# The first norm's modulation and the even layer's by matmuls on quarters of TensorE's columns, and two directions' scores on halves of its rows

## The chip, the cores and the metric

The kernel runs on one core of a Trainium2 chip. The metric is the device time of one execution in microseconds, taken as the median of several runs. The core has five engines that work side by side, each through its own instructions in their order: TensorE (PE), which multiplies a stationary block of weights of up to 128x128 with moving columns and writes to PSUM, VectorE (DVE), ScalarE (ACT), GpSimd (POOL) and SyncE (SP), which here issues all transfers between DRAM and the on-chip memory. An instruction that waits for another engine or for a transfer holds up all that is behind it on its engine.

## The reference

One step of a small trunk with two layers over 128 context tokens (tile 0 of the kernel) and 512 latent tokens (tiles 1 to 4), 1024 features, all in float32. The even layer has gated linear attention (GLA) and retention heads, the odd one latent attention; each is followed by a squared-ReLU MLP. Every norm is modulated: a shift, a scale and a gate come from the conditions `c` (latents) and `c_ctx` (context).

```python
def ada_mod(cond, w_ada, b_ada):
    m = jnp.einsum('bd,de->be', jax.nn.silu(cond), w_ada) + b_ada
    return jnp.split(m[:, None, :], 6, axis=-1)       # shift, scale, gate of the mixer; the same of the MLP

def pre_norm_mod(x, g, shift, scale):
    return rms_norm(x, g) * (1.0 + scale) + shift
```

So for each of 2 layers x 6 parts a vector of two conditions by 1024 features meets a matrix of 1024 x 1024: much weight to load, little to compute. In a chunk of a GLA head, with decayed queries and keys of 64 features, the scores are masked by direction:

```python
        a = jnp.where(causal_in_chunk, jnp.einsum('bhik,bhjk->bhij', q_dec, k_inv), 0.0)
        o = jnp.einsum('bhik,bhkv->bhiv', q_dec, S) + jnp.einsum('bhij,bhjv->bhiv', a, vi)
```

The scan runs forward and backward, each direction with its own decays, and the two outputs are added.

## The kernel before

Tokens lie in five tiles of 128. A product in float32 accuracy is made of three one-pass products: each operand is split into two summands (`hi`, `lo`; in the trace `wh` and `wl` for weights, and two `hT` for the normed, transposed input), and `mm3` issues hi x hi, hi x lo and lo x hi. Splitting a block of weights takes a copy on ACT and a subtraction on POOL or DVE. Some small products are done in plain float32 in one instruction, which the trace shows as two records, each with its own weight load.

The order of every engine's instructions is fixed when the program is written out. The kernel's parts are generators ("threads"). Class `Weave` runs them against a rough clock for each engine: `Engine.way` gives each instruction a duration from its size, and `_issue` gives a free engine the instruction of the lowest priority number, then the one that could have started longest ago. What it assumes decides only the order; on the chip an engine takes its instructions in that order and waits where an operand is late. SP's queue is filled in the same way, so a transfer that has to wait for room holds up those behind it. All instructions are emitted from one line (266 before the change), so groups in the trace are told apart by the names of their tiles.

The start. `ada_first` makes the first shift and scale (parts 0 and 1), in two halves of 512 features. `FIRST_LOADS` orders the loads: 16 of w_ada (`rada`, 256 rows x 512 columns each, scale and shift in turn), the tiles of x, and the first weights. PE takes all rows of the shift and the last four blocks of 128 rows of the scale: matmuls with four columns of weights (`wide`, the conditions among zeros) and 512 moving columns of w_ada. DVE takes the scale's first four blocks (`FIRST_ON_VECTOR`), as running sums `ada` on 128 partitions for each condition, which PE then sums by columns of ones. The four rows of the result go by ACT into `row`, four transposes put them on columns, and DVE makes `mod` of them. Behind each half `pre_norm` scales the transposed tiles (`h`, `hT`), and `gemm_first` begins the even layer's first product (bank `pg`) on that half of the features, for all five tiles, and then on the second half.

The even layer. `gemm_nat` makes the product's seven groups of columns, one after another, tile by tile. For each tile a `tile_thread` takes the banks as they come: gates and decays (`gk`, `la`, `pos`, `tri`), decayed queries and keys `qt` and `kt`, the masked scores, sums and states, GLA's gate `ga`, then retention (`dup`, `qk`, `qr`, `kr`) and its gate `gb`. For the GLA scores the forward direction's 64 features lie on the first 64 partitions and the backward ones on the other 64. For each direction four matmuls (one for each head) on 64 rows fill a bank, and DVE copies it under the mask (`copy_predicated`).

Beside it the thread `modulations` makes the parts that come next: `ADA_EVEN` are the even layer's gate and the MLP's shift and scale, (0,2), (0,3) and (0,4). Each has two halves; for each half `ada_half` has 16 DVE operations on 128x512 (`ada<-rada,cT,ada`), two for each block of 128 rows, and `ada_cols` two transposes and two sums on DVE, one PE matmul with `fold` (tile `pc<-sums,fold`), four small ACT copies and `mod`. The loads for it (`rada`, 256 KB) have two slots in the even layer. The other parts, `ADA_MLP` and `ADA_LAST`, are made in the same way beside the two MLPs.

`out_proj` is the even layer's output product with its norm and residual (`y`, `x`), and the MLP follows.

Of the kernel before, what the change touches and what calls it, by code (L numbers as in the profile page):

```python
# [11 lines left out]
F32 = mybir.dt.float32  # L12
# [7 lines left out]
P = 128  # L20
# [15 lines left out]
NCONST = 1320  # L36


def _constants():
# [4 lines left out]
    # running sums of log decays over a tile, taken from its middle (the 1/16 of the gate is in here)  # L44
# [20 lines left out]
    c[:, C_FOLD:] = j % 32 == np.arange(32)  # L65
# [4 lines left out]
# The parts of the kernel are generators that emit instructions; they are interleaved by a rough  # L70
# clock per engine, so that each engine's instructions come in the order in which their operands do.
# [5 lines left out]
class Slots:  # L77
    """The tiles of a tag (or of several pools), handed out and given back."""
# [16 lines left out]
class Weave:  # L95
    """Each thread's instructions come in their order; an engine that is free takes, of those that could start,
    the one of the lowest priority number, then the one that has waited longest (the vector engine: the
    one of the oldest thread)."""
# [55 lines left out]
    # the order  # L154
# [9 lines left out]
    def _at(self, th, eng):  # L164
        """When what the thread's next instruction needs is there."""
# [6 lines left out]
    def _end(self, th, eng, us):  # L172
        """When that could be through on this engine, behind those that go first."""
# [4 lines left out]
    def _advance(self, th):  # L178
        """To the thread's next instruction, or to what it waits for."""
# [30 lines left out]
    def _issue(self, eng, start):  # L210
# [3 lines left out]
        # rather idle for a moment than be in the way of what is more urgent  # L214
# [43 lines left out]
class Engine:  # L258
    """An engine of nc whose instructions also move its rough clock."""
# [38 lines left out]


class Either:  # L300
    """Whichever of some engines is through with it first."""
# [20 lines left out]
class Trunk:  # L322
# [31 lines left out]
    def at_last(self, left, do):  # L354
        """do() when the last of left[0] comes here."""
# [11 lines left out]
    def split(self, hi, lo, src, eng=None):  # L367
        """src == hi + lo, both in the tensor engine's one-pass float32 format."""
# [9 lines left out]
    def rsqrt(self, m, r, t, scale, post=1.0):  # L378
        """r = post * (scale * m) ** -0.5, with a Newton step behind exp(-ln / 2)."""
# [13 lines left out]
    def weight(self, src, shape, lo="vector", pair=False, quota=None, room=None, prio=1):  # L393
        """To be brought in as its two summands, in the order of these calls."""
# [4 lines left out]
    def weights(self):  # L399
        """Their loads; weight_rooms() finds room for the summands."""  # L400
# [64 lines left out]
    def gemm_nat(self, units, n, out, ready=None, done=None):  # L465
        """One group of columns, tile by tile of tokens: sets out[t] to the bank."""
# [20 lines left out]
    def gemm_first(self, units, n, out, ready):  # L487
        """The same, all tiles with the first half of the rows, then all with the second."""
# [25 lines left out]
    def ada_loads(self, parts, slots, nk=1, ahead=16, after=None):  # L514
        """The rows of w_ada behind ada_half(), nk * 128 at a time."""
# [39 lines left out]
    def ada_cols(self, l, sec, half, acc, res, room=None):  # L555
        """The sums over all rows, on columns."""
# [10 lines left out]
        nc.tensor.matmul(ps[0:32, 0:32], self.fold, sm.rearrange("p c b -> p (c b)"), start=True, stop=True)  # L567
        yield
        col = sm.rearrange("p c b -> p (c b)")[:, 0:8].rearrange("p (c j) -> p c j", c=2)
        pv = ps[0:32, 0:32].rearrange("p (c j b) -> p c j b", c=2, b=4)  # L570
        for b in range(4):
            nc.scalar.copy(col[32 * b:32 * b + 32], pv[:, :, :, b])
# [52 lines left out]
    def ada_first(self, mod, halves, prepared, x_go, c_go):  # L625
        """The first shift and scale, which all else waits for, by halves of their features: the columns of w_ada
        meet cond on the tensor engine, some of its rows on the vector engine."""
        nc, w = self.nc, self.w
        res = [self.mod_tile(sec) for sec in range(2)]
        # shift's conditions in the first two columns, scale's in the next two, and columns of ones for scale's sums  # L630
        wide, hd = yield from self.take(self.tmp, [P, 512], F32, "wide")
        wide = wide[:, 0:72].rearrange("p (k c) -> p k c", c=4)
        nc.vector.memset(wide, 0.0)
        for c in range(2):
            nc.vector.memset(wide[:, 16 + c, 2 + c:3 + c], 1.0)
# [16 lines left out]
        def by_vector(half, n, done):  # L652
            acc = yield from self.ada_half(0, 1, half, 0.0, n)
            w.set(done, acc)

        w.spawn(load())
        yield prepared
        for sec in range(2):
            nc.vector.tensor_copy(wide[:, sec * KC:sec * KC + KC, sec * 2:sec * 2 + 2],
                                  self.cT.rearrange("p (c k) -> p k c", c=2))  # L660
        for half in range(2):
            ps, hp = yield from self.bank()
            row, hw = yield from self.take(self.tmp, [P, 512], F32, "row")
            n = FIRST_ON_VECTOR[half]
            done = Event()
            if n:
                w.spawn(by_vector(half, n, done))
# [8 lines left out]
            if n:  # L676
                acc = yield done
                for c in range(2):
# [1343 lines left out]
```

## Time and profile before

| | |
|---|---|
| median of 3 runs | 1617.75 us (1616.5 to 1625.09) |
| profiled execution, first to last instruction | 1615.8 us |
| PE busy | 1529.0 us (95%), 8583 records |
| PE weight loads busy | 1338.8 us (83%) |
| DVE busy | 1051.6 us (65%), 1915 instructions |
| ACT, POOL busy | 634.0 us (39%), 397.4 us (25%) |
| mean TensorE clock granted | 0.977 |
| DMA | 166.12 MB, 103 GB/s on average |

The profiled execution has no other time of its own than its span. The ends of matmuls are modelled and matmuls are pipelined, so the distance from one start to the next tells what one costs, not its own duration. In a row of the timeline the first number is the start in us from the span's beginning, the second the length in us; x2 means two records merged, and what stands in brackets is the idle time of the engine before it and what ended it. In a row of groups the numbers behind the bar are the sum in us and the mean in ns of one, then the idle time before them. The engines' waits give the sum in us, the number and the longest.

### The profile page before, as it was taken

How to read it: one execution, taken by the hardware profiler on the slowest of the kernel's cores; microseconds unless marked ns; L12 is line 12 of the kernel's file. 1: busy time of each engine (PE TensorE's matmuls, PEld its weight loads, DVE VectorE, ACT ScalarE, POOL GpSimd, SP SyncE). 2: the span in 40 equal slices, each digit the busy share in tenths (PEclk: the TensorE clock that was granted, in tenths of full speed). 3: DMA queues.
4: the chain of work that ended last, by engine and by line, in shares of the span. 5: the costliest groups of instructions: out<-in, count | busy, mean ns of one | idle time of the engine just before them, and what ended most of it. 6: DMA issues, size and time to landing. Idle time of an engine off the chain costs nothing. (4 is left out here: it accounts for less than half of the span.)

```text
span 1615.8 us, 22873 instructions
## 1 busy us (share of the span) xinstructions
PE 1529.0 (95%) x8583; PEld 1338.8 (83%) x8583; DVE 1051.6 (65%) x1915; ACT 634.0 (39%) x1485; POOL 397.4 (25%) x317
## 2 busy tenths in 40 slices
PE   5999988889999999999997989999899999999997
PEld 1587767777888998998896989998799989988996
DVE  5577898885577778768748788884766333333335
ACT  2473433354532322332235556664543223222332
POOL 2423644432111211211136320012212112111213
PEclk9999999999999999999998999999999999999999
DMA  8323423333265454445322301113344222222211
GB/s 307 106 64 109 121 85 114 102 117 96 73 178 163 143 147 142 137 144 150 116 61 84 97 21 27 40 40 118 104 130 130 72 74 68 90 79 66 78 53 65
DMA packets 146733, 166.12 MB, mean 103 GB/s; under 512 B 12112, under 2 KB 92480, under 8 KB 146624
## 3 DMA queue, kind: packets, MB, share of 16 engines
q1 hardware_dynamic: 146624, 164.68, 33.8%
q8 instruction: 67, 1.10, 0.3%
q14 instruction: 42, 0.34, 0.1%
HBM read 158.69 MB, written 5.96 MB: 102 GB/s over the span
## 5 line engine op out<-in xcount | busy, mean ns | idle before, releaser
L266 PE MATMUL p<-hT,wh 128*128 128x256 f32 (+1 forms) x2048 | 444.3, 309 | 0.0
L266 PE MATMUL p<-wh,hid 128*128 128x512 f32 x1280 | 401.8, 392 | 0.0
L266 PEld LDWEIGHTS p<-hT,wh 128*128 128x128 f32 x2048 | 342.6, 188 | 1.4
L266 PE MATMUL p<-hT,wl 128*128 128x256 f32 (+1 forms) x1024 | 316.6, 309 | 0.0
L266 POOL TENSOR_TENSOR r<-r 128x384 f32<-128x384 f32 (+1 forms) x128 | 133.6, 1044 | 725.8 <-ACT hid L266 725.8
L266 PEld LDWEIGHTS p<-wh,hid 128*128 128x128 f32 x1280 | 241.8, 189 | 49.2
L266 PE MATMUL pg<-wh,hT 128*128 128x512 f32 (+3 forms) x840 | 269.4, 394 | 3.9 <-ACT hT L266 3.5
L266 ACT CAST wh<-raw 128x1024 fp32r<-128x1024 f32 (+3 forms) x169 | 172.3, 1026 | 251.2 <-PE p L266 243.3
L266 PE MATMUL p<-wl,hid 128*128 128x512 f32 x640 | 251.1, 392 | 0.0
L266 DVE SCALAR_TENSOR_TENSOR ada<-rada,cT,ada 128x512 f32<-128x512 f32 x292 | 238.7, 859 | 2.6 <-DMA rada<-in_w_ada 2.4
L266 DVE TENSOR_TENSOR wl<-raw,wh 128x1024 fp32r<-128x1024 f32 x121 | 148.3, 1225 | 89.5 <-ACT wh L266 88.3
L266 PEld LDWEIGHTS p<-hT,wl 128*128 128x128 f32 x1024 | 193.4, 189 | 0.2
L266 PEld LDWEIGHTS pg<-wh,hT 128*128 128x128 f32 x840 | 158.0, 194 | 37.9 <-issue 8.1
L266 DVE TENSOR_TENSOR y<-y,p 128x512 f32<-128x512 f32 x140 | 95.9, 685 | 104.7 <-PE p L266 104.5
L266 DVE TENSOR_TENSOR hid<-r,hid 128x384 fp32r<-128x384 f32 (+1 forms) x128 | 63.9, 500 | 152.6 <-POOL r L266 152.6
L266 ACT ACTIVATE r<-p 128x384 f32<-128x384 f32 (+1 forms) x128 | 56.1, 439 | 266.5 <-PE p L266 266.3
L266 POOL TENSOR_TENSOR wl<-raw,wh 128x1024 fp32r<-128x1024 f32 (+3 forms) x44 | 105.1, 2400 | 211.1 <-ACT wh L266 184.0
L266 PE MATMUL pg<-wl,hT 128*128 128x512 f32 (+3 forms) x360 | 145.8, 405 | 1.1 <-POOL wl L266 1.1
L266 PEld LDWEIGHTS p<-wl,hid 128*128 128x128 f32 x640 | 120.9, 189 | 24.2
L266 PEld LDWEIGHTS pg<-wl,hT 128*128 128x128 f32 x360 | 70.2, 195 | 16.3 <-issue 2.6
L266 ACT ACTIVATE hid<-r 128x384 fp32r<-128x384 f32 (+1 forms) x128 | 60.4, 472 | 2.2
L266 PE MATMUL ps<-kn,qn 128*128 128x320 f32 (+1 forms) x216 | 49.7, 311 | 1.4 <-ACT prob L266 1.4
(259 smaller groups left out, 2013.8 us busy)
## 6 DMA issues: line engine op xcount, KB each, us to landing
raw<-in_w_mlp SPq DMA_DIRECT2D x128, 512.0 KB, 4.2
rada<-in_w_ada SPq DMA_DIRECT2D x160, 256.0 KB, 2.9
rada<-in_w_ada SPq DMA_DIRECT2D x16, 512.0 KB, 5.4
raw<-in_w_in_even SPq DMA_DIRECT2D x16, 512.0 KB, 3.7
x<-in_x_sample SPq DMA_DIRECT2D x8, 512.0 KB, 7.7
gate<-gate SPq DMA_DIRECT2D x8, 512.0 KB, 4.6
raw<-in_w_out_even SPq DMA_DIRECT2D x8, 512.0 KB, 3.9
raw<-in_w_out_odd SPq DMA_DIRECT2D x8, 512.0 KB, 4.2
```

The lines of the kernel that those rows point to most:

```text
L266: emit = lambda: real(*a, **k)
```

## The change

Three things are changed.

First, the modulation in `ada_first` and that of `ADA_EVEN` no longer use DVE for the products. `wide` is now a constant tile of 34 columns for each block of rows, with the two conditions in columns 2 and 3 and zeros elsewhere. A window of 32 columns puts the conditions on rows 0 and 1 or on rows 2 and 3 of a quarter of the bank. `ada_four` issues four float32 matmuls in one piece, for four blocks of rows, each into another 32 partitions of the same bank, and so on another quarter of PE's columns. A half of a part takes two such batches, a half of the first shift and scale four. `ada_turned` copies the whole bank to `row` and adds the quarters up with four matmuls by `fold`, which is now 128 columns wide (ones where the row and column agree by 32). The loads of the even layer's parts have four slots and no longer two.

Second, the scores of both directions, eight matmuls on 64 rows, are issued in one piece, head by head with the two halves of the rows in turn, into two banks. The masked copies follow.

Third, the room for DVE's running sums (`pada`) is taken within the MLPs alone. `ada_cols`, which the MLPs still use, follows the wider `fold`. The order of all instructions is planned anew, with 1.4 us assumed for a batch of `ada_four` and 2.2 us for eight scores.

```diff
+    def batch(self, fn, calls, us):
+        ways = [self.way(fn, a, k) for a, k in calls]
+        self.w.put((self.name, us, lambda: [x[2]() for x in ways]))
...
+    def ada_four(self, ps, rows, start, stop):
+        self.nc.tensor.batch("matmul", [
+            ((ps[32 * j:32 * j + 32], self.wide[:, kc, 2 - 2 * sec:34 - 2 * sec], raw), dict(start=start, stop=stop))
+            for j, (raw, kc, sec) in enumerate(rows)], 1.4)
+
+    def ada_turned(self, ps, n, row):
+        nc = self.nc
+        nc.scalar.copy(row, ps)
+        yield
+        for j in range(4):
+            nc.tensor.matmul(ps[:, n * j:n * j + n], row[:, j * P:(j + 1) * P], self.fold[:, 0:n], start=True, stop=True)
+        yield
+
+    def ada_tensor(self, l, sec, half, res):
+        ps, hp = yield from self.bank()
+        for k0 in (0, 4):
+            got, held = [], []
+            for kc in range(k0, k0 + 4):
+                raw, hr = yield self.ada_ev[l, sec, half][kc]
+                got.append((raw, kc, 0))
+                held += hr
+            self.ada_four(ps, got, k0 == 0, k0 == 4)
+            self.drop(*held)
+            yield
+        row, hr = yield from self.take(self.tmp, [P, 512], F32, "row")
+        yield from self.ada_turned(ps, 2, row)
+        self.drop(hr)
+        self.mod_cols(l, sec, res[:, :, half * 4:half * 4 + 4], half * 4,
+                      ps[:, 0:8].rearrange("p (j c) -> p c j", c=2))
+        self.drop(hp)
...
         for half in range(2):
+            if (l, sec) in ADA_EVEN:
+                yield from self.ada_tensor(l, sec, half, res)
+                continue
             acc = yield from self.ada_half(l, sec, half, rest)
             yield from self.ada_cols(l, sec, half, acc, res)
...
-            todo = [(sec, kc) for kc in range(KC) for sec in range(2) if sec == 0 or kc >= n]
-            # one group for all columns of the bank
-            for sec, kc in todo:
-                raw, hr = yield self.ada_ev[0, sec, half][kc]
-                nc.tensor.matmul(ps[0:4], wide[:, sec * KC + kc], raw, start=(sec, kc) == todo[0],
-                                 stop=n == 0 and (sec, kc) == todo[-1])
-                self.drop(*hr)
+            todo = [(k0, sec) for k0 in (0, 4) for sec in (1, 0)]
+            for i, (k0, sec) in enumerate(todo):
+                got, held = [], []
+                for kc in range(k0, k0 + 4):
+                    raw, hr = yield self.ada_ev[0, sec, half][kc]
+                    got.append((raw, kc, sec))
+                    held += hr
+                self.ada_four(ps, got, i == 0, i == 3)
+                self.drop(*held)
                 yield
-            if n:
-                acc = yield done
-                for c in range(2):
-                    nc.tensor.matmul(ps[0:4], wide[:, 16 + c], acc[c], start=False, stop=c == 1)
-                yield
-            nc.scalar.copy(row[0:4], ps[0:4])
-            for j in range(4):
-                nc.tensor.transpose(ps[:, 4 * j:4 * j + 4], row[0:4, j * P:(j + 1) * P], self.ident[0:4, 0:4])
-            yield
+            yield self.cols_ready
+            yield from self.ada_turned(ps, 4, row)
...
-        self.ada_later(ADA_EVEN, self.slots(ph, "erada", 2))
+        self.ada_later(ADA_EVEN, self.slots(ph, "erada", 4))
...
+            pas = []
+            for _ in range(2):
+                pas.append((yield from self.bank()))
+            rows_ = [slice(d * 64, d * 64 + 64) for d in range(2)]
+            cols_ = [slice(h * P, (h + 1) * P) for h in range(NH)]
+            nc.tensor.batch("matmul", [((pas[d][0][:, c], kt[r, c], qt[r, 0, c]), dict(start=True, stop=True))
+                                       for c in cols_ for d, r in enumerate(rows_)], 2.2)
+            yield
             for d, M in ((0, A), (1, B)):
-                r = slice(d * 64, d * 64 + 64)
-                pa, hp = yield from self.bank()
-                for h in range(NH):
-                    s = slice(h * P, (h + 1) * P)
-                    nc.tensor.matmul(pa[:, s], kt[r, s], qt[r, 0, s], start=True, stop=True)
-                yield
-                nc.vector.copy_predicated(h4(M), masks[:, d].unsqueeze(1).broadcast_to((P, NH, P)), h4(pa))
-                self.drop(hp)
+                nc.vector.copy_predicated(h4(M), masks[:, d].unsqueeze(1).broadcast_to((P, NH, P)), h4(pas[d][0]))
+                self.drop(pas[d][1])
                 yield
```

More of the change, by code (lines that the diff above doesn't have):

```diff
@@ L35 @@
     0, 128, 256, 384, 512, 640, 768, 896, 1024, 1152, 1280, 1288)
-NCONST = 1320
+NCONST = 1416
 def _constants():
@@ L64, in _constants @@
     c[64:, C_POS + 3] = 1.0 / 16.0
-    c[:, C_FOLD:] = j % 32 == np.arange(32)
+    c[:, C_FOLD:] = j % 32 == i % 32
     return c
@@ L566, in ada_cols @@
         ps, hp = yield from self.take(self.psg if room else self.psum, [P, 512], F32, "pc")
-        nc.tensor.matmul(ps[0:32, 0:32], self.fold, sm.rearrange("p c b -> p (c b)"), start=True, stop=True)
+        nc.tensor.matmul(ps[:, 0:32], self.fold, sm.rearrange("p c b -> p (c b)"), start=True, stop=True)
         yield
         col = sm.rearrange("p c b -> p (c b)")[:, 0:8].rearrange("p (c j) -> p c j", c=2)
-        pv = ps[0:32, 0:32].rearrange("p (c j b) -> p c j b", c=2, b=4)
+        pv = ps[:, 0:32].rearrange("p (c j b) -> p c j b", c=2, b=4)
         for b in range(4):
-            nc.scalar.copy(col[32 * b:32 * b + 32], pv[:, :, :, b])
+            nc.scalar.copy(col[32 * b:32 * b + 32], pv[32 * b:32 * b + 32, :, :, b])
         self.drop(hp)
@@ L629, in ada_first @@
         res = [self.mod_tile(sec) for sec in range(2)]
-        wide, hd = yield from self.take(self.tmp, [P, 512], F32, "wide")
-        wide = wide[:, 0:72].rearrange("p (k c) -> p k c", c=4)
-        nc.vector.memset(wide, 0.0)
-        for c in range(2):
-            nc.vector.memset(wide[:, 16 + c, 2 + c:3 + c], 1.0)
+        nc.vector.memset(self.wide, 0.0)
         def load():
@@ L650, in load @@
             w.set(self.loaded)
-        def by_vector(half, n, done):
-            acc = yield from self.ada_half(0, 1, half, 0.0, n)
-            w.set(done, acc)
         w.spawn(load())
         yield prepared
-        for sec in range(2):
-            nc.vector.tensor_copy(wide[:, sec * KC:sec * KC + KC, sec * 2:sec * 2 + 2],
-                                  self.cT.rearrange("p (c k) -> p k c", c=2))
+        nc.vector.tensor_copy(self.wide[:, :, 2:4], self.cT.rearrange("p (c k) -> p k c", c=2))
         for half in range(2):
@@ L663, in ada_first @@
             row, hw = yield from self.take(self.tmp, [P, 512], F32, "row")
-            n = FIRST_ON_VECTOR[half]
-            done = Event()
-            if n:
-                w.spawn(by_vector(half, n, done))
-            todo = [(sec, kc) for kc in range(KC) for sec in range(2) if sec == 0 or kc >= n]
-            for sec, kc in todo:
-                raw, hr = yield self.ada_ev[0, sec, half][kc]
-                nc.tensor.matmul(ps[0:4], wide[:, sec * KC + kc], raw, start=(sec, kc) == todo[0],
-                                 stop=n == 0 and (sec, kc) == todo[-1])
-                self.drop(*hr)
-                yield
-            if n:
-                acc = yield done
-                for c in range(2):
-                    nc.tensor.matmul(ps[0:4], wide[:, 16 + c], acc[c], start=False, stop=c == 1)
-                yield
-            nc.scalar.copy(row[0:4], ps[0:4])
-            for j in range(4):
-                nc.tensor.transpose(ps[:, 4 * j:4 * j + 4], row[0:4, j * P:(j + 1) * P], self.ident[0:4, 0:4])
-            yield
+            todo = [(k0, sec) for k0 in (0, 4) for sec in (1, 0)]
[7 more added lines that the diff above has]
+                self.drop(*held)
+                yield
+            yield self.cols_ready
+            yield from self.ada_turned(ps, 4, row)
             pv = ps[:, 0:16].rearrange("p (j s c) -> p s c j", s=2, c=2)
-            yield self.cols_ready
             for sec in range(2):
@@ L692, in ada_first @@
             self.drop(hp, hw)
-        self.drop(hd)
     def pre_norm(self, t, x, xn, sm, mods, ready, halves=None, lo="gpsimd"):
@@ L776, in run @@
         self.pmod = self.pool(ctx, "mod", 2)
-        self.pada = self.pool(ctx, "ada", 1)
         self.sm = self.slots(ctx, "small", 20)
@@ L791, in run @@
         self.ident = const("ident", [P, P])
-        self.fold = const("fold", [P, 32])
+        self.fold, self.wide = const("fold", [P, P]), const("wide", [P, KC, 34])
         self.cT, self.cols = const("cT", [P, 16]), const("cols", [P, 160])
@@ L885, in main @@
                 load(post[16:32], k_rows("norm_mlp_post")),
-                load(self.fold, io["consts"][:, C_FOLD:C_FOLD + 32]), then=lambda at: w.set(arrived2, None, at))
+                load(self.fold, io["consts"][:, C_FOLD:C_FOLD + P]), then=lambda at: w.set(arrived2, None, at))
         yield arrived
@@ L985, in mlp @@
         NB = FF // 512
+        self.pada = self.pool(ph, f"ada{l}", 1)
         self.ada_later(ADA_MLP if l == 0 else ADA_LAST, self.slots(ph, f"rada{l}", 4))
@@ L1971 @@
 FIRST_LOADS = "aacaaaxaawaxaxaaxaaxaaa"
-FIRST_ON_VECTOR = (4, 4)
 ADA_EVEN = [(0, 2), (0, 3), (0, 4)]
```

## The prediction

> **What bounds the kernel now.** I read the page first, then the busy time by stretch, then what TensorE (PE) waits for.
>
> ```profile
> span 1615.8 us, 22873 instructions
> ```
>
> ```profile
> 0.00:64.00 64.00, 46.29 (x118) 12.62 (x119) 31.85 (x78) 17.66 (x35) 18.43 (x16) 0.95 0.71 237
> 64.00:440.00 376.00, 341.45 (x1798) 286.14 (x1796) 285.79 (x470) 173.08 (x404) 146.67 (x103) 0.94 0.33 97
> 440.00:1610.00 1170.00, 1141.28 (x6671) 1040.05 (x6669) 731.62 (x1364) 443.20 (x1046) 231.60 (x198) 0.99 0.33 97
> ```
>
> After the stretch come its length and busy us of PE, weight load, VectorE (DVE), ScalarE (ACT) and GpSimd (POOL), then PE's clock, the DMA share and GB/s. PE sets the end everywhere. The change lies in the first two stretches: the start (first norm) and the even layer with its output product. There PE stands idle for 376 - 341.45 = 34.5 us and runs at 0.94 of its clock. The rest of the program is left as it is, and its 28.7 idle us with it. So a microsecond won or lost before 440 should arrive at the end.
>
> ```profile
> PE ps L266 <- DVE dup L266: 11.0, 2, 6.4
> PE pc L266 <- DVE sums L266: 8.3, 2, 5.6
> PE ps L266 <- DVE y L266: 5.7, 1, 5.7
> PE ps L266 <- DVE mod L266: 3.4, 1, 3.4
> PE ps L266 <- DVE gk L266: 2.1, 1, 2.1
> PE ps L266 <- DVE gb L266: 1.8, 1, 1.8
> ```
>
> These are PE's waits in 64 to 440 (us, times, longest): 32.3 of the 34.5, all on DVE. `sums` and `mod` are the modulation itself; `dup`, `gk` and `gb` are the layer's own work, queued on DVE behind it:
>
> ```profile
> 249.56 6.55 DVE L266 SCALAR_TENSOR_TENSOR ada<-rada,cT,ada 128x512 f32<-128x512 f32 x3
> ...
> 262.08 0.45 PE L266 MATMUL ps<-ident,dup 128*128 128x128 f32 x1 [4.56 <-DVE dup L266]
> 262.18 0.77 PE L266 MATMUL pg<-wh,hT 128*128 128x512 f32 x1
> ```
>
> ```profile
> 214.00:229.00 15.00, 8.59 (x37) 6.67 (x37) 12.54 (x28) 5.32 (x16) 4.45 (x2) 0.77 0.35 105
> 400.00:412.00 12.00, 6.31 (x25) 4.84 (x24) 6.02 (x12) 5.31 (x13) 4.24 (x2) 0.72 0.55 181
> 107.00:140.00 33.00, 33.00 (x179) 27.40 (x179) 25.14 (x37) 18.26 (x52) 14.59 (x13) 0.84 0.33 100
> ```
>
> A long stall costs twice, since the clock falls with it: the two stretches around a stall (clock 0.77 and 0.72) lack 15 x 0.23 = 3.45 and 12 x 0.28 = 3.4 us of full clock, the first and last of five such stalls. About 1 us of each falls into the idle time, so I price the slow resumption at 2.4 us, five times: 12 us. Stretch 107 to 140 lacks another 5.3 us with no idle time; the scores lie there.
>
> **The change, part by part.**
>
> *DVE in the even layer.* Six halves of gate, shift and scale leave it.
>
> ```profile
> 64.00:400.00 336.00, 0.00 (x0) 0.00 (x0) 104.94 (x108) 0.94 0.33 98
> ```
>
> ```profile
> L266 DVE TENSOR_REDUCE sums<-tr 128x16 f32<-128x512 f32 x12 | 8.2, 680 | 0.2
> ```
>
> The first row holds the partial sums and transposes, the second what sums them up. 113 us of DVE go, two fifths of its work in the stretch. They hid behind PE, so they are worth only the stalls they caused: `sums` 8.3 for certain (the instruction is gone); of `dup`, `gk` and `gb` (14.9) I take 12; of `mod` and `y` (9.1), whose chains stay, 3.7. Sum **-24** (bounds -8.3 and -32). With them goes the slow clock behind four of the five long stalls, 9.6, and from the scores' stretch I take 1.4 of 5.3: **-11** (bounds -5 and -17).
>
> *What PE gets for it.* A half becomes two batches of four fp32 matmuls, each with 32 columns of weights and 512 moving, then four small ones by `fold`: 12 batches and 24 small ones. The nearest rows are the first scale's matmuls with four columns, between wide ones:
>
> ```profile
> 53.29 0.48 PE L266 MATMUL pg<-wh,hT 128*128 128x480 f32 x1
> 53.70 1.02 PE L266 MATMUL ps<-rada,wide 128*4 128x512 f32 x2
> 54.66 0.49 PE L266 MATMUL pg<-wl,hT 128*128 128x480 f32 x1
> ```
>
> An fp32 matmul is two records, here 0.43 us each, and 0.1 on the way out (53.70 to 54.66 is 0.96). Of the 0.41 from 53.29 to 53.70 I give half to the wide matmul's 480 columns and half, 0.2, to the way in. No row shows two quarters of the columns at work together. Full overlap makes a batch 0.86 + 0.32 = 1.18 us, none 3.44 + 0.32 = 3.76. If the second record of one matmul holds up the first of the next, five record lengths remain, 2.15 + 0.32 = 2.47. I take 1.8, midway between full overlap and this chain, since the quarters share no rows of output: 12 x 1.8 = 21.6 us.
>
> [...]
>
> ```profile
> 117.31 0.28 PE L266 MATMUL ps<-pos,la 128*128 128x2 f32 x2
> 117.45 0.36 PE L266 MATMUL pg<-wh,hT 128*128 128x256 f32 x1
> 117.65 0.28 PE L266 MATMUL ps<-pos,la 128*128 128x2 f32 x2
> ```
>
> A fold matmul has the shape of `pos,la`: 0.34 from one to the next, less some 0.12 for the 256 columns between them (by the 0.2 for 480), 0.22; 24 make 5.3. The six old `pc` leave, smaller still; at the same price, 1.3. Each half also puts one copy of 128x512 on ACT, and takes four small ones off; ACT is busy 173 of 376 us and covers it.
>
> *The scores.* Eight fp32 matmuls a tile on 64 rows, five tiles.
>
> ```profile
> 159.00 0.48 PE L266 MATMUL ps<-qt,kt 64*128 64x128 f32 x2
> 159.41 0.42 PE L266 MATMUL pg<-wl,hT 128*128 128x320 f32 x1
> 159.76 0.49 PE L266 MATMUL ps<-qt,kt 64*128 64x128 f32 x2
> ...
> 122.51 0.71 PE L266 MATMUL ps<-qt,kt 64*128 64x128 f32 x4
> 123.15 0.38 PE L266 MATMUL ps<-pos,la 128*128 128x2 f32 x2
> ```
>
> Between wide products one costs 0.76 less 0.15 for 320 columns, 0.61 us, 40 make 24.4. Two in a row take 0.64 together, so the second adds only about 0.23: most of the price is going in and out of the half array. Eight in a row without overlap: 0.4 + 8 x 0.23 = 2.2; with the halves alternating, nine record lengths, 1.4. I take 1.8, five make 9: **-15.4** (bounds -13.4 and -17.4). It now takes two banks at a time, and DVE's first masked copy waits for all eight; both lie behind PE's products.
>
> PE's work changes by 21.6 + 5.3 - 1.3 - 15.4 = **+10** (bounds 1 and +36: 12 x 1.18 with 17.4, 12 x 3.76 with 13.4).
>
> *The start.*
>
> ```profile
> 22.11 1.06 ACT L266 ACTIVATE junk<-x 128x1024 bf16<-128x1024 f32 x1 [3.74 <-DMA x<-in_x_sample]
> ```
>
> ```profile
> 27.81 1.88 PE L266 MATMUL ps<-ada,wide 128*4 128x512 f32 x4
> ...
> 30.99 0.16 DVE L266 TENSOR_TENSOR mod<-ps,cols 128x8 f32<-128x8 f32 x1
> ...
> 37.21 0.48 PE L266 MATMUL pg<-wh,hT 128*128 128x480 f32 x1 [3.48 <-ACT hT L266]
> ```
>
> The eighth load of w_ada was issued ahead of this x, so it was there by 22.1; PE needed until 29.7 for its backlog. With the last batch alone left, the first half's modulation comes some 5 us earlier, and the first product (37.21) too. The second half's 14 matmuls, 1.37 (53.29 to 54.66) - 0.2 = 1.17 us each between products, were some 16 us of PE's time; four batches are 7: 9 less. Both together would be 14, but the last x tiles and two late loads arrive by their own time. I take **-9** (bounds -3 and -14).
>
> *New waits.* A batch waits for four loads, and all of PE's products stand behind it, where before DVE waited. The loads stand in SP's queue, among the even weights:
>
> ```profile
> SPq L266 <- DVE ada L266: 153.0, 41, 17.2
> SPq L266 <- POOL wl L266: 94.6, 18, 27.7
> ```
>
> The first row, SP held up by DVE, becomes a wait for PE, with four slots and not two. The second stays, on average 5.3 us. PE did not lack weights behind either, so there is slack; I put half a microsecond on a batch: **+6** (bounds 0 and +64, that mean wait at every batch).
>
> Sum: -24 - 11 + 10 - 9 + 6 = -28. The span becomes 1588; the runs' median of 1617.75 stands 2 us above this span, for what lies around it: **1590 us**.
>
> **The rivals.**
> 1. *The quarters and halves don't run together.* Batches at 3.76, scores at 2.2: PE's work +36 and the start -3: -24 - 11 + 36 - 3 + 6 = +4, about **1622**. For it: no row shows overlap. Against: the drains around single score matmuls go anyway.
> 2. *DVE stays late.* Three of its operations take 6.55 us at 249.56, twice the group's mean (last row below): something beside their number stretches them, and may stretch what stays. Then only `sums` goes, with two slow clocks: -8 - 5 + 10 - 9 + 6 = -6, **1612**.
> 3. *All of it works*: full overlap, every DVE stall but half of `y` gone, start -14, no new wait: PE +1 - 30 - 14 - 14 = -57, **1561**.
> 4. *Slower: PE waits for w_ada.* A load of a batch is behind a weight load that waits for POOL, and PE stops at the batch. If every second batch catches one mean wait of 5.3 and a slow clock of 2.4, 6 x 7.7 = 46 replaces the 6: +12, **1630**. It decides from some 35 us in all, 3 us a batch. For it: a batch's loads can be issued only when the batch before it is through. Against: DVE waited for w_ada in 64 to 400 for only 2.4 us:
>
> ```profile
> L266 DVE SCALAR_TENSOR_TENSOR ada<-rada,cT,ada 128x512 f32<-128x512 f32 x84 | 89.9, 1100 | 2.6 <-DMA rada<-in_w_ada 2.4
> ```
>
> but at a slower pace, with loads far ahead.
>
> **How the numbers follow.** Forecast 50%, with its own range 1575 to 1604; overlap missing 10%; DVE stays late 15%; all works 15%; PE waits for loads 10%. The range, 1560 to 1620, leaves out the fourth rival, the upper half of the first and a third of the third, 20% in all. Half a per cent, 8 us, is what a measurement here tells from no change. Faster: forecast, third rival and half of the second, with a little of the first, 0.76; same: the rest of the second and most of the first, 0.14; slower 0.10.
>
> **What would show it.** The six fold matmuls `pc` of the even layer are gone, PE's waits on `dup` are under 3 us, and DVE's time in 64 to 400 is down by over 100. Twelve groups of `rada,wide` matmuls take 1.2 to 2.5 us each from the record ahead to the one behind; 3.8 means rival 1. A tile's scores come in one piece of about 1.8 us. The first `pg` starts near 32. PE waits of 3 us and more on `DMA rada` mean rival 4. I am wrong if the even layer's end moves by less than 10 us with DVE relieved, or if the gain is made and lost again behind 440.

## The result, and the profile after

| | before | changed |
|---|---|---|
| median | 1617.53 us (1616.5 to 1625.09, 4 runs) | 1582.17 us (1579.54 to 1583.79, 4 runs) |
| profiled span | 1615.8 us | 1579.4 us |

The ratio is 0.9765 (95% interval 0.9743 to 0.9786): about 2.3% faster, 35 us between the medians. The forecast was 1590 us, 8 above the measured median, with 1560 to 1620 as its range. One execution on record is slow, that of e3's profile (2151 us at a mean clock of 0.65): it has no part in e3's ratio, and its trace isn't used.

The busy time by stretch of the changed kernel has the columns of the prediction's table (PE, weight load, DVE, ACT, POOL, then clock, DMA share, GB/s):

```profile
0.00:64.00 64.00, 37.73 (x179) 20.27 (x180) 22.44 (x58) 23.14 (x50) 20.14 (x17) 0.86 0.73 248
64.00:440.00 376.00, 362.81 (x2073) 301.83 (x2072) 205.49 (x386) 183.90 (x399) 136.08 (x105) 0.98 0.36 110
440.00:1570.00 1130.00, 1103.78 (x6483) 1011.52 (x6481) 702.60 (x1322) 426.02 (x1015) 229.48 (x194) 0.99 0.32 95
```

From 64 to 440, DVE has lost 285.8 - 205.5 = 80 us, PE's idle time has fallen from 34.5 us to 376 - 362.81 = 13.2, and PE's clock has risen from 0.94 to 0.98. Behind 440 PE's idle time is much as before (28.7 us up to 1610 then, 26.2 up to 1570 now). These are PE's waits in 64 to 440:

```profile
PE ps L266 <- DVE y L266: 5.7, 1, 5.7
PE ps L266 <- DVE dup L266: 5.0, 1, 5.0
PE ps L266 <- DMA rada<-in_w_ada: 1.9, 2, 1.1
PE ps L266 <- ACT vb L266: 0.4, 1, 0.4
PE ps L266 <- DVE kr L266: 0.2, 1, 0.2
```

Of the waits on DVE before, `sums`, `mod`, `gk` and `gb` are gone and one of two on `dup`; the one on `y` is as it was. Waits for w_ada came in, 1.9 us in all by this view; the part on the prediction says what it leaves out.

Where the time went is seen from when PE reaches the same work. The first weight load of the output product (`pg<-wo`) closes the even layer. Before:

```profile
368.12 2.06 PEld L266 LDWEIGHTS pg<-wo,hT 128*128 128x128 f32 x9
```

Changed:

```profile
331.88 3.23 PEld L266 LDWEIGHTS pg<-wo,hT 128*128 128x128 f32 x14
```

It comes 36.2 us earlier, and the span ends 36.4 earlier. So, but for 0.2 us, all of the gain is made in the start and the even layer, and none of it is lost behind.

### The profile page after: what moved, and what is told of

Read it like the earlier page. It is cut to its first block, busy times and chain, and to the rows that moved or that the text cites. A ratio compares the mean times of both kernels' runs of the same rounds, so it can differ in the third digit from the quotient of the medians.

```text
span 1579.4 us, 22994 instructions
## 1 busy us (share of the span) xinstructions
PE 1504.5 (95%) x8731; PEld 1333.6 (84%) x8731; DVE 935.8 (59%) x1776; ACT 634.2 (40%) x1467; POOL 387.3 (25%) x317
## 4 chain that ended last, share of the span: by engine, by line
PE 61%; issue 23%; DVE 7%; POOL 4%; ACT 2%; DMA 1%; SPq 0%; POOLq 0%; DVEq 0%; ACTq 0%
PE p L266 29%; PE pg L266 18%; PE ps L266 12%; POOL r L266 4%; DVE sm L266 3%; PE pqk L266 2%; DMA rada<-in_w_ada 1%; PE pv L266 1%; DVE x L266 1%; DVE y L266 1%; ACT junk L266 1%; DVE xn L266 0%; ACT prob L266 0%; DVE rope L266 0%; ACT wh L266 0%
## 5 line engine op out<-in xcount | busy, mean ns | idle before, releaser
L266 PE MATMUL pg<-wh,hT 128*128 128x512 f32 (+3 forms) x840 | 264.0, 389 | 0.0
L266 DVE TENSOR_TENSOR wl<-raw,wh 128x1024 fp32r<-128x1024 f32 x121 | 148.2, 1225 | 93.0 <-ACT wh L266 92.7
L266 POOL TENSOR_TENSOR wl<-raw,wh 128x1024 fp32r<-128x1024 f32 (+3 forms) x44 | 100.3, 2294 | 216.4 <-ACT wh L266 181.5
L266 PE MATMUL pg<-wl,hT 128*128 128x512 f32 (+3 forms) x360 | 141.6, 393 | 0.0
L266 DVE SCALAR_TENSOR_TENSOR ada<-rada,cT,ada 128x512 f32<-128x512 f32 x196 | 139.3, 758 | 0.0
```

Source lines behind the costliest of these rows:

```text
L266: emit = lambda: real(*a, **k)
```

## The experiments

Each of the twelve kernels was timed beside the kernel before on the same chip. "us by ratio" below is the difference of two ratios to before, times 1618; its uncertainty is 4 to 6 us.

| run | median us | ratio to before (95%) |
|---|---|---|
| changed kernel | 1582.2 | 0.9765 (0.9743 to 0.9786) |
| e1 scores apart | 1604.4 | 0.9920 (0.9894 to 0.9946) |
| e2 even layer's modulation on DVE | 1605.6 | 0.9923 (0.9904 to 0.9942) |
| e3 first norm as before | 1589.7 | 0.9830 (0.9803 to 0.9857) |
| e4 one quarter | 1609.4 | 0.9947 (0.9927 to 0.9967) |
| e5 scores in turn | 1585.8 | 0.9783 (0.9766 to 0.9799) |
| e6 DVE loaded | 1601.3 | 0.9879 (0.9862 to 0.9895) |
| e7 before, with the new scores | 1603.9 | 0.9898 (0.9882 to 0.9915) |
| e8 lower summands on either engine | 1548.6 | 0.9555 (0.9536 to 0.9574) |
| e9 the same, input weights alone | 1561.0 | 0.9637 (0.9617 to 0.9657) |
| e10 before, with e8's edit | 1576.3 | 0.9727 (0.9707 to 0.9746) |
| e11 e8 and the odd layer | 1547.7 | 0.9547 (0.9527 to 0.9568) |
| e12 e8 and the first norm | 1554.2 | 0.9588 (0.9565 to 0.9612) |

The first four take back one part each.

### e1: the scores apart

```diff
-            nc.tensor.batch("matmul", [((pas[d][0][:, c], kt[r, c], qt[r, 0, c]), dict(start=True, stop=True))
-                                       for c in cols_ for d, r in enumerate(rows_)], 2.2)
...
             for d, M in ((0, A), (1, B)):
...
+                r = slice(d * 64, d * 64 + 64)
+                pa, hp = yield from self.bank()
+                for h in range(NH):
+                    s = slice(h * P, (h + 1) * P)
+                    nc.tensor.matmul(pa[:, s], kt[r, s], qt[r, 0, s], start=True, stop=True)
...
```

> The changed kernel with the scores of layer 0 in the form of before: four matmuls of one direction, then four of the other, each with a place of its own in the order. Theory A (the two row halves run beside each other; in the changed kernel's trace a tile's eight scores take 1.1 us in all, before each took 0.61 us): 5 tiles x (8 x 0.61 - 1.1) = +19 us, so about 1601 us. Theory B (the prediction's term, 15.4 us): about 1597 us. Rival (the scores stood in time in which PE would have waited anyway, so the piece is worth little): under +5 us, below 1587 us.

Measured: 22 us slower than the changed kernel by the medians, 25 by ratio. That rules out the rival and the 15.4, and is a little more than theory A's 19. In the changed kernel, a tile's eight scores with what stands behind them:

```profile
143.28 1.16 PE L266 MATMUL ps<-qt,kt 64*128 64x128 f32 x16
144.37 0.38 PE L266 MATMUL ps<-fold,row 128*128 128x2 f32 x2
```

143.28 to 144.37 is 1.1 us for eight, and so in all five tiles, against 8 x 0.61 = 4.9 before: 5 x 3.8 = 19. The clock differs too. The stretch 107 to 165, where the scores lie, in e1:

```profile
107.00:165.00 58.00, 58.00 (x310) 41.67 (x310) 20.55 (x35) 19.61 (x52) 17.99 (x18) 0.85 0.41 131
```

and in the changed kernel:

```profile
107.00:165.00 58.00, 58.00 (x458) 48.23 (x457) 30.73 (x49) 28.20 (x67) 27.09 (x22) 1.00 0.55 177
```

PE is busy all the time in both, with no wait. Yet with scores scattered among the wide products the clock is 0.85, and 58 x 0.15 = 8.7 us of full clock are missing. 19 and 8.7 make more than the 22 to 25 measured, so the two overlap; how much each is worth alone isn't shown.

### e2: the even layer's modulation back on DVE

```diff
-            if (l, sec) in ADA_EVEN:
-                yield from self.ada_tensor(l, sec, half, res)
-                continue
...
-        self.ada_later(ADA_EVEN, self.slots(ph, "erada", 4))
+        self.pada = self.pool(ph, "adae", 1)
+        self.ada_later(ADA_EVEN, self.slots(ph, "erada", 2))
```

> The changed kernel with the even layer's modulation back on VectorE (two slots for its rows, as before); the first norm and the scores stay changed. Theory A (stalls and the slow clock behind them come back, -21 and about -12 us of the changed kernel, against 18 us of new PE work in that layer that goes away): +7 to +18 us, 1589 to 1600 us, with waits of PE for DVE's dup, gk, gkT in the even layer again. Rival 1 (what the even layer's part brings is all of the gain that the start and the scores don't explain, and its PE work is hidden): +25 us or more, over 1607 us. Rival 2 (start and scores are the whole gain, the new PE work eats what the stalls give): within 4 us of the changed kernel, 1578 to 1586 us.

Measured: 23 us slower by the medians, between theory A and rival 1, and 26 by ratio, which rival 1 has. The waits say what theory A left out. PE in 64 to 360:

```profile
PE ps L266 <- DVE dup L266: 11.0, 2, 6.4
PE pc L266 <- DVE sums L266: 8.5, 3, 5.6
PE ps L266 <- DVE ee L266: 6.0, 2, 4.2
PE ps L266 <- DVE mod L266: 3.1, 1, 3.1
PE pg L266 <- POOL wl L266: 2.7, 2, 2.0
PE ps L266 <- DVE gk L266: 2.4, 2, 1.5
PE ps L266 <- DVE gb L266: 1.8, 1, 1.8
```

The stalls of before are back, some to the tenth (`dup` 11.0, `gb` 1.8), and `ee`, in the scores' stage, is new: PE is through with the short scores sooner and finds DVE late. Until the first `dup` (207.4 in e2, 207.6 in the changed kernel) PE's new work costs what those stalls do; the 21 us are made after it, where in the changed kernel the modulation has long been finished.

### e3: the first norm as before

The old `ada_first` is put back: columns on PE, four rows of the scale on DVE; the sums lie in a `y` tile.

> The changed kernel with the first norm's modulation in the old form (columns on PE, four rows of each half of scale on VectorE; the sums lie in a y tile). Theory A (the start's gain stays to the end): first pg about 2 us and the end of the first group some 10 us later, +8 to +12 us, 1590 to 1594 us. Rival (the first groups wait for loads and for the norm of x, not for this): below +4 us, under 1586 us.

Measured: 7.5 us slower by the medians, 10.5 by ratio, about what theory A has. Without a trace, only the sum can be compared.

### e4: one quarter of the columns

```diff
-            ((ps[32 * j:32 * j + 32], self.wide[...], raw), dict(start=start, stop=stop))
+            ((ps[0:32], self.wide[...], raw), dict(start=start and j == 0, stop=stop and j == 3))
...
-        nc.scalar.copy(row, ps)
+        nc.gpsimd.memset(row, 0.0)
+        nc.scalar.copy(row[0:32], ps[0:32])
```

> The changed kernel with all four matmuls of a batch into the same 32 columns of TensorE, one sum, instead of four quarters: the same count of matmuls, no overlap of quarters; the copied row is 32 partitions high, the other 96 are zeroed by GpSimd. Theory A (four quarters overlap fully, 1.07 us per batch; without that 4 x 0.94 = 3.8 us): 12 batches of the even layer x 2.7 = +32 us, and up to 10 us at the start, 1612 to 1625 us. Rival (the overlap is of no weight, because the batches stand where PE waits): below +10 us, under 1592 us.

Measured: 27 us slower (29 by ratio). The mechanism is theory A's; the time is 3 us below its range. A batch in e4:

```profile
95.56 3.62 PE L266 MATMUL ps<-rada,wide 128*32 128x512 f32 x8
99.11 0.50 PE L266 MATMUL ps<-wg,gkT 98*128 98x512 f32 x1
```

and in the changed kernel:

```profile
42.28 0.38 PE L266 MATMUL pg<-wl,hT 128*128 128x480 f32 x1
42.59 1.07 PE L266 MATMUL ps<-rada,wide 128*32 128x512 f32 x8
43.58 0.49 PE L266 MATMUL pg<-wh,hT 128*128 128x480 f32 x1
```

99.11 - 95.56 = 3.55 us against 43.58 - 42.59 = 0.99: the quarters overlap fully, 2.56 us a batch, 31 for twelve. From the start of each batch to what follows it, the even layer's twelve take 44 us in all in e4 and 18 in the changed kernel, where some wait for their loads (see *New waits* below), so 26 are left of the 31. The start is later too: the first `pg` comes at 41.0 and not at 35.2. Part of it all comes back, since e4 has no wait for `dup` any more (5.0 in the changed kernel): a later PE finds DVE ready.

### e5: four scores of one half, then four of the other

```diff
-                                       for c in cols_ for d, r in enumerate(rows_)], 2.2)
+                                       for d, r in enumerate(rows_) for c in cols_], 2.2)
```

> The changed kernel with a tile's eight scores still in one piece, but four of the one row half and then four of the other, not by turns. Theory A (the two row halves run beside each other): alone a 128-column f32 matmul takes about 0.23 us at full clock, so a piece takes 8 x 0.23 + 0.2 = 2.1 us in place of 1.1 us: +5 us, 1587 us, and in its trace four records of one half stand one behind the other. Rival (what is saved is the way in and out of the half-row form between other matmuls, once per piece and not per score; the halves don't matter): 1.1 to 1.3 us per piece, within 1 us of the changed kernel, 1581 to 1584 us.

Measured: 3 us slower by ratio, which the times can't tell from nothing. The trace can:

```profile
137.41 1.71 PE L266 MATMUL ps<-qt,kt 64*128 64x128 f32 x16
139.04 0.42 PE L266 MATMUL pg<-wh,hT 128*128 128x320 f32 x1
```

1.63 us for the piece, and so in all five tiles, between the theories. So of the 3.8 us saved on a tile, 4.9 - 1.63 = 3.3 come from issuing the eight together and 0.5 from the two halves running side by side.

### e6: DVE loaded

```diff
...
+        def load_dve():
+            yield mod[0, 1]
+            yield 5.0
+            for i in range(48):
+                for c in range(6):
+                    nc.vector.scalar_tensor_tensor(self.idle[0], self.idle[0], self.cT[:, c:c + 1], self.idle[0],
+                                                   op0=ALU.mult, op1=ALU.add)
+                yield 4.5
...
+        w.spawn(load_dve(), None, 1)
```

> The changed kernel with 288 operations more on VectorE in the even layer (on a tile of 128 x 176 zeros, in 48 bursts; about what was taken from it, some 90 us), whose result nobody uses and for which nobody waits. Theory A (VectorE's time alone is what made the late dup, gk, gkT, ee): those waits come back beside the new PE work, +15 to +34 us, 1597 to 1616 us. Rival (the stalls came of the modulation's own chain: its loads on SP's queue, its sums, its banks): within 4 us of the changed kernel, below 1587 us.

Measured: 19 us slower (18 by ratio), as theory A has it. In the trace 206 of the 288 operations lie between 64 and 440 and take 126 us, rather more than was meant: half of them take 402 ns or less, but their mean is 612, so many are stretched (e10 shows by what). PE waits again, at other places in part:

```profile
213.13 0.45 PE L266 MATMUL ps<-ident,dup 128*128 128x128 f32 x1 [6.75 <-DVE sm L266]
294.85 0.79 PE L266 MATMUL ps<-kr,qr 128*128 128x128 f32 x2 [7.59 <-DVE kr L266]
388.32 0.69 PE L266 MATMUL ps<-ident,y 128*128 128x128 f32 x2 [7.44 <-DVE y L266]
```

No load, no sum and no bank of the modulation is in this: more work on DVE, beside GpSimd's as it was, is enough to make stalls.

### e7: the kernel before, with the new scores alone

The edit is e1's in the other direction, on the kernel before.

> The kernel before with the scores in one piece by turns, the modulation left as it was. Theory A (beside VectorE's old load the time that PE saves is lost again in waits for VectorE: the run with only the modulation of the even layer taken back was 13 us below the kernel before, of which the start has 7.5): -3 to -8 us, 1610 to 1615 us, with waits for ee in the scores' stage. Rival (additive: scores are worth on the kernel before what their undoing cost, 22 us): 1596 to 1600 us.

Measured: 16.5 us faster than before (ratio 0.9898), between the two ranges and nearer to the rival's. Theory A's mechanism is there:

```profile
118.41 0.48 PE L266 MATMUL ps<-ident,ee 128*128 128x128 f32 x1 [3.98 <-DVE ee L266]
129.25 0.33 PE L266 MATMUL ps<-ident,ee 128*128 128x128 f32 x1 [0.79 <-DVE ee L266]
138.62 0.42 PE L266 MATMUL ps<-ident,ee 128*128 128x128 f32 x1 [2.05 <-DVE ee L266]
```

6.8 us of new waits, taken from the 22 to 25 that the same edit is worth beside a relieved DVE. The scores and the relief of DVE help each other, which is why e1 and e2 each cost most of the gain.

### e8 and e9: lower summands on whichever engine is free

In the changed kernel one wait for `dup` was left. GpSimd just before it:

```profile
202.84 2.35 POOL L266 TENSOR_TENSOR wl<-raw,wh 128x1024 fp32r<-128x1024 f32 x1
```

and DVE:

```profile
202.97 2.24 DVE L266 TENSOR_SCALAR sm<-sm 128x4 f32<-128x4 f32 x1
205.72 0.36 DVE L266 TENSOR_TENSOR sm<-sm 128x4 f32<-128x4 f32 x2 [0.51 <-ACT sm L266]
```

Four elements a partition take 2.24 us, and both operations end together (205.19 and 205.21). e8 lets the order choose the engine for the even layer's input and output weights and for the first block of each MLP (the last line is run for both MLPs):

```diff
-        self.u_in_even = self.nat_units(io["w_in_even"][0], EVEN_GROUPS, "gpsimd", prio=0)
+        self.u_in_even = self.nat_units(io["w_in_even"][0], EVEN_GROUPS, "either", prio=0)
...
-            lo = "vector" if b else "gpsimd"
+            lo = "vector" if b else "either"
```

> The changed kernel with the lower summands of the even layer's input, output and first MLP weights computed by whichever of VectorE and GpSimd is through first, not by GpSimd alone. Theory A (a small VectorE operation beside a long GpSimd one takes 2.2 us and the last dup comes 5.0 us late; VectorE has room now): -3 to -8 us, 1574 to 1579 us. Rival 1 (lower summands on VectorE delay its own chains as the modulation did): +5 us or more. Rival 2 (the order finds GpSimd first in nearly all cases): within 2 us, 1580 to 1584 us.

Measured: 1548.6 us, 34 us below the changed kernel, four times and more what theory A expected; no rival comes near either. The even layer in e8:

```profile
64.00:440.00 376.00, 374.80 (x2211) 319.21 (x2210) 230.02 (x446) 187.38 (x410) 73.85 (x75) 1.00 0.38 120
```

GpSimd falls from 136 to 74 us, DVE rises from 205 to only 230 although it now does most of those subtractions, and PE is idle for 1.2 us at full clock. Not all of the 34 us are the even layer's: e8 is 17 us ahead of the changed kernel at the first output product (314.8 against 331.9), 25 at the odd layer's output product (1051.6 against 1076.8) and 32 at the end of the profiled span. The last 7 lie in the second MLP, where PE's wait for `y` falls from 5.7 us to 1.1.

e9 takes the first of these edits alone.

> The changed kernel with the lower summands of the even layer's input weights alone (not the output's, not the MLP's) on whichever of VectorE and GpSimd is through first. In the run with all three, PE's first dup came 12 us sooner, the first output product 17 us, the end 32 us. Theory A (each set brings what its stage showed): the input weights alone -12 to -17 us, 1565 to 1571 us, and the 5.7 us wait for y at the end of the even layer stays. Rival (the gain of all three hangs together, because a stage that comes sooner is only late behind the next one's GpSimd work): under -5 us, above 1577 us.

Measured: 1561.0, 21 us below the changed kernel, somewhat more than theory A had; the wait for `y` stays (5.6 us), as it said. The remaining 13 us are the other two sets': in the traces e9 is no later than e8 at the first output product (313.0 against 314.8), 4 us later at the odd layer's output product and 11 at the end, so 7 are the second MLP's.

### e10: the same edit on the kernel before

> The kernel before with the same three sets of lower summands on whichever engine is through first. Theory A (the room on VectorE is what the change made; beside the modulation's 90 us the order leaves them on GpSimd or makes VectorE later still): -8 to +10 us, 1608 to 1628 us, far from the 33 us that it brings on the changed kernel. Rival (GpSimd was a bound of its own in both kernels): -25 us or more, below 1594 us.

Measured: 1576.3 us, 44 us below the kernel before and 6 below the changed one (about the uncertainty). Theory A falls, and the time is the one that the rival expected. But GpSimd was no bound by itself: in the kernel before PE waited for `wl` from GpSimd for only 1.1 us between 64 and 440. In e10 the modulation is still DVE's:

```profile
64.00:440.00 376.00, 366.63 (x1954) 306.76 (x1953) 294.14 (x534) 186.81 (x426) 80.38 (x74) 0.97 0.38 111
```

DVE is busier than in any other of these kernels but e6 (294 us, 286 before) and PE's idle time is 9.4 us, where it was 34.5. So it wasn't DVE's amount of work alone that made it late. Groups of DVE in the kernel before, 64 to 400 (behind the bar: sum, mean ns):

```profile
L266 DVE SCALAR_TENSOR_TENSOR ada<-rada,cT,ada 128x512 f32<-128x512 f32 x84 | 89.9, 1100 | 2.6 <-DMA rada<-in_w_ada 2.4
L266 DVE TENSOR_SCALAR sm<-sm 128x4 f32<-128x4 f32 x20 | 8.5, 426 | 0.6
L266 DVE SCALAR_TENSOR_TENSOR ga<-ps,sm,ga 128x128 f32<-128x128 f32 x20 | 6.0, 342 | 0.4
```

and in e10:

```profile
L266 DVE SCALAR_TENSOR_TENSOR ada<-rada,cT,ada 128x512 f32<-128x512 f32 x84 | 69.4, 850 | 5.7 <-DMA rada<-in_w_ada 5.7
L266 DVE SCALAR_TENSOR_TENSOR ga<-ps,sm,ga 128x128 f32<-128x128 f32 x20 | 5.9, 343 | 0.4
L266 DVE TENSOR_SCALAR sm<-sm 128x4 f32<-128x4 f32 x20 | 5.8, 291 | 0.4
```

The same 84 operations of the modulation take 20 us less, the small ones a third less, and those that read a bank of PSUM (`ga<-ps`) as long as before.

The whole stretch from 64 to 400 says the same when each DVE operation is compared with the fastest of its kind (same operation, tiles and shape). In the kernel before, the 92 without an operand in PSUM that overlap a GpSimd operation in time take 72 us more than that in all, and the 169 that overlap none take 2 us more; the 29 with an operand in PSUM that overlap one take 0.4 us more (the ten reductions and transposes that overlap one take 0.1 us more in all and are left out). The 72 us are 40 in the changed kernel, 29 in e10 and 15 in e8.

### e11 and e12: further in the same direction

> The changed kernel with the three sets on whichever engine is first, and the odd layer's weights too. Theory A (what it is about is GpSimd's load in the even layer; the odd layer's GpSimd is busy 61 us of 200): within 4 us of the run with three sets, 1545 to 1553 us. Rival (the odd layer's waits for y, sm and qs come of GpSimd too): -5 us or more, below 1544 us.

Measured: 1547.7 us, within 1 us of e8, as theory A has it: in the odd layer the choice is worth nothing that these runs can tell.

> The changed kernel with the three sets on whichever engine is first, and the lower summand of the first norm too. Theory A (the 2 to 6 us that PE waits for xn at the start go, because GpSimd no longer runs beside the long VectorE operations): -2 to -6 us from the run with three sets, 1543 to 1547 us. Rival (VectorE is as late with its own work there): within 2 us, or slower, 1547 us or more.

Measured: 1554.2 us, 5.5 slower than e8 and 6.4 slower than e11, beside which it ran: the rival's number. But the edit changes a default that also holds for the norm behind the first MLP, and the traces put most of the loss there. e12 reaches the even layer's first `gk` at 72.7 (e8: 74.3) and the first output product at 315.9 (315.0), but the odd layer's first product at 820.0 (817.0) and its output product at 1056.2 (1051.6). For the first norm's summand by itself the run shows no more than 1 us either way.

e8 and e11 can't be told apart, and both beat the kernel before (by about 72 us) and the changed one (by 34). The change and e8's edit are worth 38 and 44 us alone on the kernel before and 72 together, by the ratios: mostly separate gains.

## Why the prediction was right, point by point

*PE is what counts, and what is won before 440 arrives at the end.* Held: 36.2 us at the output product, 36.4 at the end.

*DVE's stalls, -24.* PE's idle time in 64 to 440 fell by 21.3, and its waits for DVE by 22 (from 33 to 11); e2 and e6 show that DVE's time made the stalls. The reason given was half of it, though. "Queued on DVE behind it" names the modulation as the cause, and e10 shows that DVE can do all of it with few stalls (9.4 us of idle time) when GpSimd does less beside it. Before one of the two went, both were needed. Rival 2 had the clue, "something beside their number stretches them", and it was right that the cause stays: the wait for `dup` kept 5.0 us of 11.0, where under 3 were forecast. DVE's time in 64 to 400 fell by 83 us (262.1 to 179.1) and not by over 100: the 113 us went, but the window now holds 36 us more of the MLP's stage. Up to 364, as far as 400 was before, it is 156.8 us, 105 less.

*The slow clock behind the stalls, -11.* The stretch 64 to 440 lacked 376 x 0.06 = 22.6 us of full clock before and 376 x 0.02 = 7.5 after, 15 less. Three of the five long stalls went; less about 1 us of each that falls into idle time, as the prediction counted, 12 remain. The size held, but the split didn't: three stalls at 2.4 make 7.2 and not 9.6, and from the scores' stretch only 1.4 was taken, where all 5.3 came (107 to 140 now has a clock of 1.00).

*PE's work, +10.* The term that was mis-sized; it is about -3. The step that failed is "I take 1.8, midway between full overlap and this chain": a batch whose loads are there takes 1.0, full overlap, so twelve cost 12 and not 21.6 (the waits for loads are counted below). The chain, in which the second record of one matmul holds up the first of the next, doesn't occur: the first records of a batch's four matmuls start at 111.089, 111.096, 111.102 and 111.109, some 7 ns apart, and the second ones from 111.542. A tile's scores take 1.1 and not 1.8: 24.4 - 5.5 = 19 saved in place of 15.4. Twenty-four fold matmuls at 0.22 were right (113.07 to 113.41 is again 0.34 from one to the next, with a product of 256 columns between). 12 + 5.3 - 1.3 - 19 = -3.

*The start, -9.* Right in sum (e3: 7.5 to 10.5), wrong in its course. The first `pg` was to start near 32 and starts at 35.2, 2 us sooner than before, since PE waits for the norm of x there, and that norm is itself held up beside a subtraction on GpSimd (at 27.56 the same operation takes 0.74 us):

```profile
32.26 2.21 POOL L266 TENSOR_TENSOR wl<-raw,wh 128x960 fp32r<-128x960 f32 x1
32.35 2.67 DVE L266 TENSOR_SCALAR xn<-x,sm 128x1024 f32<-128x1024 f32 x1
35.07 0.48 PE L266 MATMUL ps<-ident,xn 128*128 128x128 f32 x1 [5.60 <-DVE xn L266]
```

The rest came in the first product: its last matmul starts at 84.8, before 89.3, with three batches of the even layer's modulation already done.

*New waits, +6.* Right in size, though the view of waits has only 1.9 us for w_ada behind 64. The matmuls of a batch wait one by one, each for its own load. The batch at 86.48 takes 4.1 us to the next product, and PE counts as busy for much of it:

```profile
86.48 1.71 PE L266 MATMUL ps<-rada,wide 128*32 128x512 f32 x4 [1.06 <-DMA rada<-in_w_ada]
88.98 1.70 PE L266 MATMUL ps<-rada,wide 128*32 128x512 f32 x4 [0.79 <-DMA rada<-in_w_ada]
90.61 0.39 PE L266 MATMUL pg<-wh,hT 128*128 128x256 f32 x1
```

The batch at 73.54 takes 2.3 us in the same way, those at 139.42 and 146.62 take 1.5 each. With the 1.06 us ahead of 86.48 that is 6.4 us over 1.0 a batch. (The one at 64.81 takes 1.9 at a clock of 0.50, and the other seven 1.0.) Rival 4, 46 us of such waits, is out; all of the modulation was through by 158.

*The sum.* -22 - 12 - 3 - 9 + 6 = -40, and 36 came. The terms aren't independent: e7 shows the scores' saving eaten in part by waits for DVE in the kernel before. Which rows hold the 4 us between isn't settled. The mechanism was right but for the reason of DVE's lateness; that the forecast of -28 comes within 8 us of -36 is in part luck, because PE's work was 13 us off, and the 4 us that no row explains make up for some of it.

*Rival 1* is settled by the traces (0.99 and 1.1 us). What it would have cost is shown in part: e4, without the quarters' overlap but with the scores at 1.1, takes 1609 us. With the 5.5 us of scores at 2.2 that would be some 1615, an estimate, where rival 1 had 1622. *Rival 3*'s full overlap came, but not the rest of it: a wait for `dup` stayed, and the start brought 9 and not 14.

## What to carry to other kernels

A wait of PE for DVE isn't priced by counting DVE's work alone: first look for long GpSimd operations that end at the same moment as a stretched DVE one, because moving these may be worth more than taking work off DVE (44 us against 38 here). Small float32 matmuls on half of PE's rows belonged in one piece here, not scattered among full-size ones: of the 3.8 us saved on a tile's scores 3.3 came from that alone (e5). When two engines are late together, undo each part of a change alone, and also do each alone; their gains need not add up (e1 and e2 each cost 22 us or more of 36). Before blaming what an edit names, see what else it touches: e8 and e12 both reach a second place.

A wait view counts PE's idle time only. A group of matmuls that wait one by one shows up as a longer group instead (4.1 us for the batch at 86.48, where 1.0 is the time without waits).

## What the runs showed of the hardware that was not expected

*DVE operations were held until GpSimd's ended.* In the kernel before GpSimd runs two subtractions at 206.35:

```profile
206.35 5.15 POOL L266 TENSOR_TENSOR wl<-raw,wh 128x1024 fp32r<-128x1024 f32 x2
```

and DVE two operations on four elements a partition:

```profile
206.87 4.65 DVE L266 TENSOR_TENSOR sm<-sm 128x4 f32<-128x4 f32 x2
```

They end at 211.50 and 211.52. The stall of 6.4 us on `dup` follows at 221.2. In 64 to 400 of the kernel before, 51 DVE operations take over 0.3 us more than the fastest of their kind, and each ends behind a GpSimd operation that it overlaps, the ten of them with eight elements a partition or fewer within 0.03 us. One operand is enough for it: the `TENSOR_SCALAR` at 202.97 in the changed kernel takes 2.24 us (the fastest of its kind 0.16), and three of ten `COPY dup<-qk` in the kernel before 0.70 (0.28). With an operand in PSUM nothing is held: `ga<-ps` keeps its 342 to 344 ns in before, changed kernel, e8 and e10 alike. Why they are held isn't shown.

*A subtraction of 128x1024 costs 2.6 us on GpSimd and 1.2 on DVE* (means of `wl<-raw,wh` in the kernel before: 2621 ns in 64 to 440 and 1225 over the whole span), so a DVE operation that waits for one from start to end loses more than the subtraction would have cost DVE.

*Four float32 matmuls on four quarters of the columns took as long as one* (0.99 us a batch; one with four columns took 0.96 before, 53.70 to 54.66, and four in one quarter take 3.55), though each is two records.

*PE's clock fell without any idle time in the records.* In 107 to 165, with PE busy but for 0.1 us at most, it is 0.91 in the kernel before, 0.85 in e1 and 0.79 in e10, where the scores are scattered, and 1.00 in the changed kernel, e5 and e8, where they stand together. In slices of 5 us it falls for a while and comes back: 0.62 to 0.70 at 110 to 115 and 125 to 135 in the kernel before, 0.50 from 120 to 140 in e10. But scattered scores aren't enough for it: 48 of the 80 score records of the kernel before lie in 135 to 165, at 1.00. What makes it fall there isn't settled.
